# A two-layer hybrid decoder trunk on one core: the gates of all three mixer branches ahead of the first branch's product

## Chip, cores and metric

One Trainium2 chip, one of its cores. The metric is the time of one execution on the device in microseconds. The kernel before was timed in three runs: 1636.29, 1632.41 and 1636.13 us, median 1636.13.

## What is computed

Two layers over 256 tokens of width 1024, each a mixer and then a mixture of experts (MoE), both with a residual. The mixer, cut to what matters here:

```
proj = h @ w_in                                   # one input projection; the last 3 x 1024 columns are the gates
y_a = diff_attention(qa, ka, va) @ w_proj_a       # branch A
y_b = conformer_conv(ub) @ w_proj_b + b_proj_b    # branch B: GLU, 31-tap depthwise conv, layer norm, swish
y_c = stick_breaking(qc, kc, vc) @ w_proj_c       # branch C: 8 heads
g = sigmoid(gates)                                # (token, branch, channel)
merged = g[0] * y_a + g[1] * y_b + g[2] * y_c
return merged @ w_out
```

The MoE sends each token to 8 of 64 experts and adds a shared expert. Which experts' weights sit in which place is known only once the router has run.

## The kernel before

Channels lie on the partitions, tokens on the free axis. A mixer's work on TensorE (PE) is, in this order: the front (the projections to q, k, v and the conv's input), then "gates" and "branches" in the order of the string `PLAN` (line 86), then the output projection, then the MoE.

- `gate(br)` (lines 1205 to 1219) computes one branch's gates: eight chunks of 128 channels by 256 tokens, 24 matmuls each, from two 2 MB weight tiles. The weights are split into a rounded and a residual part by ScalarE (ACT, line 681, `WH`) and VectorE (DVE, line 682, `WL`), two such splits a chunk in layer 0, some five pieces ahead of PE. Each pair of chunks ends in a sigmoid (line 1217) into a tile `sg`, of which there are four; the gates of the branch that comes first go into `merged` instead.
- `branch(br)` (lines 1221 to 1272) waits until the branch's output stands in `T` ("oa", "ob" or "oc"), multiplies it by the projection in four quarters, and adds gate times product to `merged` (lines 1250 to 1256). With four `sg` tiles no more than one branch beside the first can have its gates ready.
- PE's and SyncE's (SP) instructions stand in the order in which the program writes them. Those of DVE and ACT are ordered by a scheduler at build time, by priority in the program's order. Each engine works through its queue in that order.
- A planner writes the program (lines 1312 to 1348). `main()` is the mixer's backbone (gates, branches); each of its turns gives the estimated PE and DVE time of the piece just written. After each turn every "side" (attention heads, rope, the conv's norm) writes its next small piece, and "fills" are written for as long as there is credit: single taps of the conv (line 760, 124 in a layer, estimated at 0.41) and parts of the modulation's dot products (line 525, `mod`, 1.2 each), the two in turn where both are open. Credit grows by `rate` x PE time less DVE time; in layer 0 the rate is 1.2 until A's and C's attention are done, then 0.65.
- Where a branch's input isn't ready, main's turn is a `STALL` of (0.6, 0): only sides and fills are written. A gate chunk is a turn of (2.77, 1.2) in layer 0 and (3.1, 0.78) in layer 1, a quarter of A or C in layer 0 one of (3.65, 1.88).
- `attn_c` (line 1038) begins one head of C every three turns of main in layer 0, every five in layer 1; the last head needs seven turns more, and "oc" is set behind it. `conv_norm` (line 784) follows the conv's last tap over seven turns and sets "ob".
- In layer 0, by this plan, gate a and gate c end with turn 42; turns 43 to 56 are STALLs (14) in which the attention of A and C ends and 47 taps of the conv are written, 11 of them inside the norm of A's output; A is written in turns 57 to 60, C in 61 to 64, gate b in 65 to 72, B in 73 to 76. In layer 1, gate b ends with turn 46, turns 47 to 55 are STALLs (9), A is 56 to 59, B 60 to 63, gate c 64 to 71, C 72 to 75; C's last head begins in turn 63 and "oc" is set in turn 69.
- All weights come through one stream in the order of use: 2 MB tiles in five buffers, issued by SP (line 218 for the mixer, line 251 for the experts). A `mod` tile frees its buffer when its dot products are done. In layer 0 the two `mod` tiles behind gate c's are open to the fills once the next weight tile is taken.

Of the kernel before, what the change touches and what calls it, by code (L numbers as in the profile page):

```python
# [11 lines left out]
F32 = mybir.dt.float32  # L12
# [9 lines left out]
P = 128  # L22
D = 1024
KC = D // P
S = 256
# [57 lines left out]
LK = 1  # L83
GATE1 = 4
START1 = (2, 1, 2)
PLAN = ("acACbB", "abABcC")

_ROWS = [("norm_mix_g", 8), ("norm_ffn_g", 8), ("b_mod", 48), ("b_dw", 4), ("conv_ln_g", 4), ("conv_ln_b", 4),
         ("b_proj_b", 8), ("subln_g", 1), ("qn", 2), ("kn", 2), ("c", 8), ("w_dw", 4 * CW),
# [79 lines left out]
def trunk(ctx, tc, A, out, dbg=None):  # L169
# [21 lines left out]
    def bank(tag):  # L191
        if tag == "S":
            turn[0] ^= 1
            tag = f"S{turn[0]}"
        return ps.tile([P, 512], F32, name="ps" + tag, tag=tag, bufs=4 if tag == "A" else 1)
# [74 lines left out]
    for l in range(L):  # L270
        mods = [(ml, b, kh) for ml, b in MODS[l] for kh in range(2)]
        seq = [("in", n, OFF[n]) for f in FRONT[l] for n in (("uba", "ubg") if f == "ub" else (f,))]
        for br in PLAN[l]:
            if br in "abc":
# [216 lines left out]
    def c2(ap, n=2):  # L491
        return ap.rearrange("p (c t) -> p c t", c=n)
# [98 lines left out]
    def mixer_body(l, pool, before=None):  # L591
# [35 lines left out]
        else:  # L627
            order = [o + (hf,) for hf in range(2) for o in seq[:4] if (*o, hf) in pieces(o)]
            del seq[:4]
        for br in PLAN[l]:  # L630
            if br in "abc":
# [89 lines left out]
        def proj_chunk(n, c, b):  # L721
            mm_all(b[:, (c % 2) * S:(c % 2 + 1) * S], ("in", n, c), XG if n in GATES else X)
# [427 lines left out]
        def main():  # L1150
# [6 lines left out]
            for n in FRONT[l]:  # L1157
# [26 lines left out]
                else:  # L1184
                    for q in range(2):
# [8 lines left out]
                        sg = pool.tile([P, 2, S], F32, name="sg", bufs=4)  # L1194
# [6 lines left out]
            gates = {}  # L1201
            split_ = set("abc")
            done_ = [br.lower() for br in PLAN[l] if br in "ABC"]

            def gate(br):
                gates[br] = []
                for q in range(4):
                    b = bank("A")
                    for k in range(2):
                        proj_chunk(f"g{br}{q // 2}", 2 * (q % 2) + k, b)  # L1210
                        if k == 0:
                            yield GH
                    if br == done_[0]:
                        sg = merged[q // 2][:, 2 * (q % 2):2 * (q % 2) + 2]
                    else:
                        sg = pool.tile([P, 2, S], F32, name="sg", bufs=4)
                    se.activation(sg, c2(b), AF.Sigmoid)
                    gates[br].append(sg)
                    yield GH
# [53 lines left out]

            for br in PLAN[l]:
                yield from gate(br) if br in "abc" else branch(br.lower())
# [638 lines left out]
```

## Time and profile before

| | |
|---|---|
| runs | 1632.41 to 1636.29 us, median 1636.13 |
| the profiled execution | 1630.8 us, its span 1629.1 us |
| share of the span | PE 96%, weight loads 64%, DVE 46%, ACT 29% |
| from HBM | 541.23 MB, 333 GB/s over the span |
| mean granted clock of TensorE | 0.978 |

The span holds mixer 0 (to about 320 us), MoE 0, mixer 1 (about 810 to 1127 us) and MoE 1. In the windows below a row gives, for a stretch, each engine's busy time with its number of instructions, the granted clock of TensorE (1.00 is 2.4 GHz, 0.50 is 1.2 GHz), and the share and rate of the DMA engines. A busy PE may be one at the lower clock.

### The profile page before, as it was taken

To read this page: it belongs to the slowest core of one execution; us is meant where nothing else is said; L and a number is where in the kernel's file an instruction comes from. 1 tells how busy PE (TensorE), PEld (TensorE's weight loads), DVE (VectorE), ACT (ScalarE), POOL (GpSimd) and SP (SyncE) were. 2 spreads that over 40 slices of the span, in tenths; PEclk is the share of its full clock that TensorE was granted. 3 is DMA by queue.
4 is the path that set the end of the run, shared out by engine and by line. 5 is a ranking of instruction groups with operands and counts; after the bars stand their busy time and mean duration, and the time that the engine had idled before them with its cause. 6 is when DMAs were issued, how large, how long until landed. Compare 5 with 4: busy or idle time off the path is not lost. (4 is left out here: it accounts for less than half of the span.)

```text
span 1629.1 us, 25483 instructions
## 1 busy us (share of the span) xinstructions
PE 1565.4 (96%) x9710; PEld 1050.0 (64%) x9710; DVE 751.1 (46%) x1866; ACT 469.5 (29%) x911; POOL 2.9 (0%) x26
## 2 busy tenths in 40 slices
PE   6999999999999999999989999999999999999998
PEld 5999879874555454455478888898654555544544
DVE  8899988642222221212259997554322222211122
ACT  3546724421111111111143355244111111111111
POOL 0000000000000000000000000000000000000000
PEclk7999979999999999999989999899999999999999
DMA  9985319959999999999959744246699999999997
GB/s 379 385 326 200 148 56 369 385 217 372 403 412 419 411 414 416 412 419 412 412 237 373 274 178 155 95 198 259 234 357 405 412 419 412 412 417 415 417 412 309
DMA packets 99198, 543.99 MB, mean 334 GB/s; under 512 B 11136, under 2 KB 11776, under 8 KB 56064
## 3 DMA queue, kind: packets, MB, share of 16 engines
q1 hardware_dynamic: 99072, 542.32, 83.2%
q8 instruction: 78, 1.28, 0.3%
q14 instruction: 48, 0.39, 0.1%
HBM read 541.23 MB, written 1.05 MB: 333 GB/s over the span
## 5 line engine op out<-in xcount | busy, mean ns | idle before, releaser
L198 PE MATMUL psT<-w,xe 128*64 128x512 f32 (+2 forms) x1152 | 229.1, 598 | 5.9 <-DMA w<-in_w_dram 5.8
L1652 DVE TENSOR_SCALAR oT<-psG,slot 128x256 fp32r<-128x256 f32 x54 | 26.1, 484 | 404.9 <-PE psG L198 404.9
L198 PE MATMUL psA<-hH,WH 128*128 128x256 f32 x696 | 209.4, 301 | 0.5 <-ACT WH L681 0.5
L681 ACT ACTIVATE WH<-w 128x512 fp32r<-128x512 f32 (+2 forms) x272 | 148.1, 554 | 200.7 <-PE psA L198 183.0
L1695 DVE SCALAR_TENSOR_TENSOR Y<-psS,gt,Y 128x512 fp32r<-128x512 f32 x108 | 81.1, 751 | 266.6 <-ACT Y L1694 266.6
L198 PE MATMUL psA<-hH,WL 128*128 128x256 f32 x696 | 196.8, 283 | 1.3 <-DVE WL L682 1.3
L198 PE MATMUL psA<-hL,WH 128*128 128x256 f32 x696 | 196.4, 282 | 0.4 <-DVE hL L570 0.4
L198 PE MATMUL psT<-wx,xe 128*64 128x512 f32 (+2 forms) x896 | 186.5, 599 | 8.3 <-DMA wx<-in_w_dram 8.3
L682 DVE TENSOR_TENSOR WL<-w,WH 128x512 fp32r<-128x512 f32 (+2 forms) x272 | 157.2, 591 | 57.2 <-ACT WH L681 56.6
L198 PEld LDWEIGHTS psT<-w,xe 128*64 128x64 f32 (+2 forms) x1152 | 73.3, 129 | 142.5 <-issue 121.7
L198 PE MATMUL psA<-room,w 128*128 128x256 f32 x592 | 145.7, 390 | 1.1 <-ACT room L573 1.1
L198 PEld LDWEIGHTS psT<-wx,xe 128*64 128x64 f32 (+2 forms) x896 | 62.2, 130 | 124.4 <-issue 100.3
L1694 ACT ACTIVATE Y<-psS,gt 128x512 fp32r<-128x512 f32 x108 | 74.4, 689 | 221.5 <-PE psS L198 221.4
L198 PEld LDWEIGHTS psA<-hH,WH 128*128 128x128 f32 x696 | 131.8, 189 | 4.0 <-ACT WH L681 1.7
L198 PEld LDWEIGHTS psA<-hL,WH 128*128 128x128 f32 x696 | 131.9, 190 | 2.8 <-DVE hL L570 0.7
L198 PEld LDWEIGHTS psA<-hH,WL 128*128 128x128 f32 x696 | 131.7, 189 | 2.2 <-DVE WL L682 2.1
L1642 ACT ACTIVATE sl<-psT 128x256 f32<-128x256 f32 x54 | 20.7, 384 | 385.2 <-PE psT L198 385.2
L198 PEld LDWEIGHTS psA<-room,w 128*128 128x128 f32 x592 | 109.8, 194 | 17.3 <-issue 2.9
L198 PE MATMUL psA<-oT,Y 128*128 128x256 f32 x864 | 116.0, 286 | 0.8 <-ACT Y L1694 0.8
L525 DVE SCALAR_TENSOR_TENSOR w<-w,room 128x1024 f32<-128x1024 f32 x96 | 115.7, 1220 | 1.1 <-DMA w<-in_w_mod_dram 1.1
L198 PEld LDWEIGHTS psA<-oT,Y 128*128 128x128 f32 x864 | 105.7, 189 | 3.6 <-ACT Y L1694 3.4
L760 DVE SCALAR_TENSOR_TENSOR room<-room,tcol,room 128x256 f32<-128x256 f32 x240 | 104.0, 481 | 0.0
(586 smaller groups left out, 2070.7 us busy)
## 6 DMA issues: line engine op xcount, KB each, us to landing
w<-in_w_dram SPq DMA_DIRECT2D x108, 1024.0 KB, 15.6
w<-in_w_dram SPq DMA_DIRECT2D x192, 512.0 KB, 10.2
wx<-in_w_dram SPq DMA_DIRECT2D x92, 1024.0 KB, 15.0
wx<-in_w_dram SPq DMA_DIRECT2D x144, 512.0 KB, 10.2
w<-in_w_in_dram SPq DMA_DIRECT2D x56, 1024.0 KB, 8.3
w<-in_w_mod_dram SPq DMA_DIRECT2D x48, 1024.0 KB, 9.3
w<-in_w_out_dram SPq DMA_DIRECT2D x8, 1024.0 KB, 8.5
wx<-in_w_dram SPq DMA_DIRECT2D x4, 2048.0 KB, 17.0
```

Of the source, the lines that this page charges most:

```text
L198: pe.matmul(out=o, lhsT=lhsT, rhs=rhs, start=start, stop=stop, skip_group_check=True)
L525: ve.scalar_tensor_tensor(t[:, j], t[:, j], 1.0, crow, op0=OP.mult, op1=OP.mult, accum_out=modv[l][:, c:c + 1])
L681: se.activation(H[:, j:], src, AF.Copy)
L682: ve.tensor_tensor(Lo[:, j:], src, H[:, j:].bitcast(F32), op=OP.subtract)
L760: ve.scalar_tensor_tensor(yv[:, ch], hp[:, ch, w:w + S], wc, yv[:, ch], op0=OP.mult, op1=OP.add)
L1642: se.activation(sl, b[:, 0:FF], AF.Silu)
L1652: ve.tensor_scalar(oT, bg[:, 0:S], slot[:, k_:k_ + 1], None, op0=OP.is_equal)
L1694: se.activation(Y[:, hf], b, AF.Copy, scale=gt)
L1695: ve.scalar_tensor_tensor(Y[:, 2 + hf], b, gt, Y[:, hf].bitcast(F32), op0=OP.mult, op1=OP.subtract)
```

## The change

In both layers the third gate moves from ahead of the last branch's product to behind the second gate. Its four tiles get a name of their own, outside the room that holds `sg`. What is computed is the same; the stream of weights follows the new order.

```
-PLAN = ("acACbB", "abABcC")
+PLAN = ("acbACB", "abcABC")
...
                     if br == done_[0]:
                         sg = merged[q // 2][:, 2 * (q % 2):2 * (q % 2) + 2]
                     else:
-                        sg = pool.tile([P, 2, S], F32, name="sg", bufs=4)
+                        sg = pool.tile([P, 2, S], F32, name="sg" if len(gates) == 2 else "sg3", bufs=4)
```

A small letter is a branch's gate, a capital its product.

## Rows read from the trace of the kernel before

**Rows 1.** The page: the slices of 40.7 us each, busy tenths of DVE, the granted clock, and GB/s moved.
```profile
DVE  8899988642222221212259997554322222211122
PEclk7999979999999999999989999899999999999999
GB/s 379 385 326 200 148 56 369 385 217 372 403 412 419 411 414 416 412 419 412 412 237 373 274 178 155 95 198 259 234 357 405 412 419 412 412 417 415 417 412 309
```
**Rows 2.** Windows: the stretches before the experts of layer 0 and of layer 1 are known, and a stretch of MoE 0. Columns: stretch, its length, then PE, weight loads (PEld), DVE, ACT, POOL busy (x instructions), granted clock, DMA share, GB/s.
```profile
332.00:345.00 13.00, 12.77 (x76) 10.72 (x74) 10.10 (x51) 4.02 (x8) 0.00 (x0) 1.00 0.01 2
...
1138.00:1152.00 14.00, 13.78 (x80) 11.60 (x79) 11.30 (x65) 5.23 (x10) 0.00 (x0) 1.00 0.00 0
...
440.00:600.00 160.00, 157.34 (x954) 82.97 (x948) 36.60 (x84) 27.46 (x50) 0.00 (x0) 1.00 1.02 415
```
**Rows 3.** Windows of mixer 0, same columns: the end of the front with gates a and c; the tail of the attention in three parts; A and C; gate b.
```profile
137.00:201.38 64.38, 64.38 (x482) 57.47 (x483) 61.28 (x161) 48.63 (x91) 0.00 (x0) 1.00 0.39 149
201.38:209.50 8.12, 7.87 (x54) 5.92 (x52) 8.02 (x21) 5.95 (x13) 0.00 (x0) 1.00 0.01 3
209.50:215.20 5.70, 3.29 (x11) 1.75 (x11) 5.70 (x24) 3.16 (x7) 0.00 (x0) 0.50 0.01 1
215.20:227.31 12.11, 12.03 (x40) 7.40 (x41) 9.21 (x21) 2.12 (x5) 0.00 (x0) 0.53 0.00 0
227.31:256.98 29.67, 29.67 (x149) 26.39 (x148) 25.37 (x55) 4.24 (x8) 0.00 (x0) 1.00 0.54 213
256.98:279.95 22.97, 22.97 (x195) 22.94 (x194) 22.59 (x43) 11.01 (x18) 0.00 (x0) 1.00 0.95 381
```
**Rows 4.** The timeline of PE at the end of that tail: start, length, engine, line, operation, tiles and shapes, number, and in brackets the idle time before it with what ended it.
```profile
215.22 0.58 PE L968 MATMUL psT<-ident,rsy 128*4 128x128 f32 x2 [2.43 <-DVE rsy L459]
...
224.47 3.00 PE L198 MATMUL psS<-room,part 128*128 128x256 f32 x8
227.31 7.07 PE L198 MATMUL psA<-room,w 128*128 128x256 f32 x32
...
235.92 10.61 PE L198 MATMUL psA<-room,w 128*128 128x256 f32 x48
```
**Rows 5.** The timeline of DVE: the conv's last tap, the second half of A's output, and the last operation of the conv's norm.
```profile
220.93 0.48 DVE L760 SCALAR_TENSOR_TENSOR room<-room,tcol,room 128x256 f32<-128x256 f32 x1
223.09 0.75 DVE L981 SCALAR_TENSOR_TENSOR room<-room,sub,psS 128x512 f32<-128x512 f32 x1 [1.69 <-PE psS L198]
...
251.12 0.48 DVE L815 SCALAR_TENSOR_TENSOR room<-room,tcol,room 128x256 f32<-128x256 f32 x1
```
**Rows 6.** Windows from the end of gate c to the end of A's output: all instructions, the same columns as in group 3.
```profile
201.38:223.84 22.46, 19.73 (x92) 12.45 (x92) 20.64 (x61) 10.85 (x24) 0.00 (x0) 0.68 0.01 1
```
**Rows 7.** Windows of line 682 alone (the residual splits; DVE busy, x instructions, clock, DMA): over gate b.
```profile
256.98:279.95 22.97, 10.04 (x15) 1.00 0.95 381
```
**Rows 8.** Windows of line 525 alone (the dot products; two records each), the same columns: behind A's output to the end of the conv's norm, and behind that over gate b.
```profile
223.84:251.60 27.76, 9.56 (x16) 0.95 0.48 186
251.60:280.00 28.40, 14.66 (x24) 1.00 0.86 350
```
**Rows 9.** The DMA issues of SP in mixer 0 by the tensor that they read: first issue, time to the last one's end, number.
```profile
160.57 0.80 SPq L218 DMA_DIRECT2D w<-in_w_proj_a_dram  x2
176.27 0.80 SPq L218 DMA_DIRECT2D w<-in_w_proj_c_dram  x2
193.52 38.33 SPq L218 DMA_DIRECT2D w<-in_w_in_dram  x4
242.81 0.80 SPq L218 DMA_DIRECT2D w<-in_w_proj_b_dram  x2
```
**Rows 10.** Windows of mixer 1, all instructions, the columns of group 3: the tail behind gate b in two parts; A; B; gate c.
```profile
1013.40:1018.40 5.00, 4.01 (x26) 2.50 (x26) 2.68 (x5) 2.46 (x6) 0.00 (x0) 1.00 0.93 392
1018.40:1028.90 10.50, 10.33 (x46) 7.52 (x44) 3.50 (x11) 2.40 (x5) 0.00 (x0) 0.66 0.01 2
1028.90:1046.40 17.50, 17.50 (x80) 14.74 (x79) 8.41 (x21) 4.89 (x11) 0.00 (x0) 0.91 0.00 0
1046.40:1060.80 14.40, 14.40 (x116) 13.24 (x114) 12.00 (x25) 5.50 (x11) 0.00 (x0) 1.00 0.78 292
1060.80:1086.80 26.00, 26.00 (x180) 24.31 (x180) 11.52 (x21) 11.71 (x23) 0.00 (x0) 1.00 0.32 122
```
**Rows 11.** The timeline of mixer 1: PE's first 48 records of branch A, and then the steps of C's last head behind its scores: sigmoid, scans, product, copy of the transposed weights, copy of the output, its rounded part, its residual part.
```profile
1028.92 12.15 PE L198 MATMUL psA<-room,w 128*128 128x256 f32 x48
...
1060.97 0.49 ACT L1005 ACTIVATE room<-psS 128x384 f32<-128x384 f32 x1 [0.65 <-PE psS L198]
...
1061.80 1.00 DVE L1012 TENSOR_TENSOR_SCAN room<-room 128x128 f32<-128x128 f32 x2
...
1062.90 0.56 DVE L1013 TENSOR_TENSOR room<-room 128x384 f32<-128x384 f32 x1
...
1070.60 0.49 ACT L935 ACTIVATE room<-psG 128x384 f32<-128x384 f32 x1
...
1077.59 0.38 ACT L1031 ACTIVATE room<-psT 128x256 f32<-128x256 f32 x1 [0.63 <-PE psT L198]
1078.01 0.63 ACT L1233 ACTIVATE oH<-room 128x512 fp32r<-128x512 f32 x1
...
1078.67 0.69 DVE L1234 TENSOR_TENSOR oL<-room,oH 128x512 fp32r<-128x512 f32 x1 [1.39 <-ACT oH L1233]
```

## Prediction

> **What bounds the kernel now.** I read the slices first, then windows stage by stage, then single rows of the stages that the change touches. In the experts' stages memory sets the pace: there the DMA engines move some 415 GB/s and are full [rows 1, 2]. Before each of these stages lie 13 and 14 us in which nothing is moved: the buffers are full, and the stream waits to learn which experts come next [rows 2]. So a mixer that ends earlier starts the experts earlier with the same tiles in place, and a microsecond won or lost in a mixer is one in the total. I cost the mixers alone.
>
> In mixer 0, PE and DVE share the pace while gates and attention run: over gates a and c DVE is busy 61.28 of 64.38 us (95%) [rows 3]. Then gate c is out, and until A starts (201.38 to 227.31) PE has only the attention's remainder, small matmuls in chains through DVE and ACT. The clock falls to 0.50 [rows 3], and one wait alone is 2.43 us [rows 4]. Behind it A, C and gate b run with no gap. In mixer 1 the tail lies behind gate b (1013.4 to 1028.9), with 0.99 us of idle PE (5.00 less 4.01) and the clock at 0.66 [rows 10].
>
> **Layer 0.** Gate b (22.97 us [rows 3]) leaves its place behind C and is written in the first 8 of the 14 waiting turns; 6 remain.
>
> From PE: the tail's work at full clock is busy time times clock: 7.87 + 3.29 x 0.50 + 12.03 x 0.53 = 15.9 us of 25.93 [rows 3]. With gate b in it, 38.9 us in place of 48.9: a gain of 10.0, if nothing else binds.
>
> From DVE: until A's output is finished, 20.64 us of the 22.46 are busy [rows 6]; nothing of gate b's splits or of the dot products is among them beyond one record. Now come ahead of that point gate b's 16 splits, 10.04 for 15 [rows 7], so 10.7; and the two modulation tiles behind gate c, which are opened to the fills by the taking of gate b's weights and so move ahead of A: 8 dot products, 9.56 us, today behind A's output [rows 8]. Sum 20.64 + 10.7 + 9.6 = 40.9 us. At the 95% that DVE reached over gates a and c this is 43 us, at 100% 40.9; A's output is finished at 242.3 to 244.4, not 223.84 [rows 5]: 18.5 to 20.6 later. From there to A's start PE takes 3.47 us now, most of it the conv's mean at half clock (3.00 [rows 4]); at full clock half of that comes back, 1.5. A starts 17.0 to 19.1 us later, and 22.97 are gone behind C: a gain of 3.9 to 6.0. I take 4.7, nearer to the lower end, since 95% is what a row shows; that DVE and not PE decides follows from 40.9 against 38.9. Bounds: 10.0 from PE's rows; below nothing, if the conv comes late (rival 3).
>
> The engines' queues: DVE's splits wait behind taps and dot products, and PE waits for the splits; that is this sum. ACT gets 16 roundings and four sigmoids into a stretch with 10.85 of 22.46 busy [rows 6]; over gate b its whole busy time is 11.01 [rows 3], and it has room for both. SP's queue: gate b's tiles take the places that A's and C's weights have (issued at 160.57 and 176.27), A's take 193.52, and the queue is idle from there to 231 [rows 3, 9], so gate b finds its weights early. C's and B's then wait for buffers of gate b or of the dot products, freed well ahead of 245. POOL's queue gets nothing. The dot products of the next tiles, 14.66 us over gate b now [rows 8], lose that place; they take the 9.56 us that are vacated beside A and C, and the rest goes beside B and the output projection. The four extra tiles cost nothing while running: their last reader is the last branch, and the output projection lies between it and the MoE.
>
> **Matmul busy time or weight loads?** In the part from 215.20 PE is busy 12.03 of 12.11 us, its weight loads only 7.40 [rows 3]. The Trainium skill (Perfetto Trace Analysis, "Identifying the Most-Contended Engine") says that matmul busy time is a bad measure of how full PE is and that weight-load time should be read. By matmul busy time the tail could take in 2.7 us of gate b (25.93 less 7.87 + 3.29 + 12.03); by weight loads (15.07 in all) up to 10.9.
>
> **Layer 1.** Gate c (8 chunks) moves into the tail's nine waiting turns. What comes back: 0.99 us idle, 10.33 x (1 - 0.66) = 3.5 at the lower clock, and 17.50 x 0.09 = 1.6 under A [rows 10]: 6.1 us. DVE, busy 6.18 of these 15.5 us [rows 10], has room here.
>
> But gate c was also the cover for the last head of C. C's heads begin by count of turns; the last begins with the turn behind B, so its whole chain now stands ahead of branch C: sigmoid 0.49, scans 1.00, product 0.56, copies 0.49 and 0.38, split 0.63 + 0.69, sum 4.24 [rows 11], with hand-overs of 0.04 to 0.34 between rows that follow each other, say 0.5, less 0.7 for the first matmuls of C that need no late channel: 4.0 us of idle PE. PE's own part of the chain is only moved. Net +2.1. The clock may fall again there: at least nothing, at most what tail and A lose now, 3.5 + 1.6; I take 1.5, the excess of A's first 48 records (12.15 [rows 11] against 10.61 in mixer 0 [rows 4]). Net +0.6, bounds -3.0 and +2.1.
>
> **Sum.** 4.7 + 0.6 = 5.3 us. The profiled execution of 1630.8 would become 1625.5; it is 5.3 below the median of 1636.1, so from the median I forecast **1630.8**. A measurement tells 0.3% (4.9 us) from no change; the forecast lies just beyond it.
>
> **Rivals.**
> 1. *DVE gives way.* If the dot products slip behind A after all, or DVE runs denser, PE's sum holds: layer 0 gains 10.0 and layer 1 up to 2.1: 12, so 1624. For it: beside gates a and c weight loads fill 57.47 of 64.38 us (89%) [rows 3], so PE is hardly less full than DVE. Against: 95% busy, and the taps come first in program order. 0.16.
> 2. *The wait is only moved.* Layer 0 gains its lower end, 3.9, and layer 1 loses 3.0, as branch C starts behind an idle PE at 1.2 GHz: gain 1, 1635. For it: the clock fell 5 us behind gate b, in work much like the last head's [rows 10]. The Trainium skill (TensorE: Matmul & The Clock Gate, "HAM oscillation") says the same, that a PE left waiting between bursts begins the next burst at the lower clock; the trace agrees, with 0.66 and 0.91 behind that tail. With the nearby lower end of my own range this makes no change. 0.18.
> 3. *The conv comes late for B, in layer 0*: slower. Today 30 us lie between the last tap and "ob" (220.93 to 251.60 [rows 5]), and B starts 28 us after that. After the change the last tap is near 242, "ob" near 272, B near 275: 3 us to spare in place of 28. By the plan's credit the waiting turns filled 19.3 us of taps with 0.8 unused; eight gate turns give 1.2 x 2.77 - 1.2 = 2.12 each, not 0.72, so 31.3 in all, against 19.3 + 9.6 for taps and dot products: 2.4 to spare. If that fails, the taps left over fall into A's turns, where credit is 0.65 x 3.65 - 1.88 = 0.49, one tap a turn, 3.7 us of PE each: from two taps left over on B waits, from about four the sum is lost and more (14.6 late less 3 gives 11.6, less the gain of 5.3: 6 slower, with the clock's fall some 10). Time 1646. 0.16.
>
> **Chances and range.** My forecast with 3 to 8 us of gain has 0.50: 0.28 of it beyond 4.9 us, 0.22 within. Faster: 0.28 + 0.16 = 0.44. Same: 0.22 + 0.18 = 0.40. Slower 0.16. The range takes in rival 1 with 2 us for the spread of the runs, 1622, and above rival 2 and the milder half of rival 3, 1641; about 1 in 10 is left out above, under 1 in 10 below.
>
> **What would show it.** Right: gate b's matmuls from 201 on, interleaved with the attention, A's start at 243 to 247, B's at 273 to 276, no clock at 0.50 for 17 us there; dot products ahead of A; in mixer 1, A's start some 20 us later than now, and 3 to 6 us of idle PE ahead of branch C with its rows of line 1012 and 1234 as releasers. Wrong: a gap ahead of B in mixer 0 that ends on line 815; DVE under 85% busy between 201 and 245; or a time at which the experts' first load waits for buffers and not for the router.

## The result, and the profile after

The changed kernel is slower. Eight runs took 1638.18 to 1648.14 us, median 1641.97; eight of the kernel before, on the same chip, 1629.56 to 1636.29, median 1633.07. The ratio is 1.0057 (95% interval 1.0044 to 1.0070), 9 us: over the 0.3% that a measurement can tell, on the other side of the forecast, and just above the range (1622 to 1641). The profiled execution of the changed kernel took 1638.2 us, the lowest of its eight; its span is 1636.6, the mean granted clock 0.981 (before 0.978).

Windows of mixer 0 of the changed kernel, with the columns of [rows 3]: the front with gates a and c; gate b with the attention; the rest of the tail; A and C in two parts, cut where PE waits; B and the first of the output projection; the rest.

```profile
137.00:201.40 64.40, 64.40 (x482) 57.37 (x481) 61.27 (x154) 49.53 (x92) 0.00 (x0) 1.00 0.48 184
201.40:235.84 34.44, 34.44 (x258) 31.63 (x256) 32.16 (x81) 19.68 (x39) 0.00 (x0) 0.95 0.49 183
235.84:251.21 15.37, 11.56 (x41) 7.07 (x41) 11.72 (x30) 2.77 (x6) 0.00 (x0) 0.67 0.01 1
251.21:271.50 20.29, 15.87 (x83) 13.89 (x81) 18.14 (x45) 1.42 (x3) 0.00 (x0) 0.99 0.56 214
271.50:287.14 15.64, 15.64 (x69) 13.72 (x69) 12.28 (x23) 3.02 (x6) 0.00 (x0) 0.90 0.95 393
287.14:305.00 17.86, 15.84 (x126) 15.30 (x125) 16.48 (x34) 7.97 (x15) 0.00 (x0) 1.00 0.93 372
305.00:328.00 23.00, 23.00 (x187) 22.68 (x185) 9.35 (x17) 9.64 (x18) 0.00 (x0) 1.00 0.58 229
```

Up to the end of gate c nothing has moved: 64.40 us against 64.38 [rows 3]. Then gate b and the tail take 34.44 + 15.37 = 49.8 us, where the tail and gate b apart took 25.93 + 22.97 = 48.9 [rows 3]: the cover bought nothing. A and C take 35.9 us in place of 29.67 [rows 3]; that is the larger loss, 6.3 us. The mark at which a mixer ends is, here and in the expectations below, "the experts' first matmul". The matmul that the times are taken from is the spread of the MoE's norm (`psA<-dg,ones`); the shared expert's own first one stands 2.08 us behind it in both kernels. The mark comes at 331.89, 7.65 us later than before (324.24).

The timeline of PE in the changed kernel shows both places; the lines answer to [rows 4].

```profile
237.46 0.38 PE L968 MATMUL psT<-ident,rsy 128*4 128x128 f32 x2 [1.63 <-DVE rsy L459]
...
240.84 0.87 PE L930 MATMUL psG<-ident,room 128*128 128x128 f32 x3 [2.19 <-DVE room L1013]
...
246.48 3.78 PE L198 MATMUL psG<-room,part 128*128 128x256 f32 x8
...
251.21 3.72 PE L198 MATMUL psA<-room,w 128*128 128x256 f32 x16
...
256.47 10.61 PE L198 MATMUL psA<-room,w 128*128 128x256 f32 x48
271.50 1.20 PE L198 MATMUL psS<-room,ones 128*128 128x128 f32 x4 [4.42 <-DVE modA L534]
272.49 15.01 PE L198 MATMUL psA<-room,w 128*128 128x256 f32 x64
287.14 0.47 PE L198 MATMUL psA<-oH,WH 128*128 128x256 f32 x1
```

Behind gate b the waits and the half clock of the old tail are still there (the conv's mean, which was 3.00 us in [rows 4], is 3.78). Between A and C a new wait stands: 4.42 us, ahead of the four matmuls that spread the conv's norm over the channels, and after it the clock is at 0.90 on the mean of the 15.64 us up to B. C's 64 matmuls stand behind those four in PE's queue.

What PE waits for there is told by the timeline of DVE in the changed kernel. The lines of 450 to 459 are the norm's eleven steps of 0.16 us each (a reciprocal root by three Newton steps), line 481 makes the diagonal matrix that PE waits for (the profile names line 534, the instruction right behind it); 525 is a dot product, 1254 multiplies a quarter of A by its gate.

```profile
256.71 0.15 DVE L450 TENSOR_SCALAR rsv<-psT 128x2 f32<-128x2 f32 x1
...
260.21 0.69 DVE L1254 TENSOR_TENSOR room<-psA,room 128x512 f32<-128x512 f32 x1 [2.07 <-PE psA L198]
260.81 0.16 DVE L452 TENSOR_SCALAR rsy<-rsv 128x2 int32<-128x2 int32 x1
260.88 1.22 DVE L525 SCALAR_TENSOR_TENSOR w<-w,room 128x1024 f32<-128x1024 f32 x1
...
262.02 0.16 DVE L455 TENSOR_TENSOR rst<-rsy 128x2 f32<-128x2 f32 x1
262.10 1.22 DVE L525 SCALAR_TENSOR_TENSOR w<-w,room 128x1024 f32<-128x1024 f32 x1
...
263.24 0.16 DVE L457 SCALAR_TENSOR_TENSOR rst<-rst,rsv 128x2 f32<-128x2 f32 x1
263.31 1.22 DVE L525 SCALAR_TENSOR_TENSOR w<-w,room 128x1024 f32<-128x1024 f32 x1
...
264.46 0.16 DVE L459 SCALAR_TENSOR_TENSOR rsy<-rst,rsy 128x2 f32<-128x2 f32 x1
...
270.93 0.42 DVE L481 TENSOR_TENSOR room<-ident,rsy 128x256 f32<-128x256 f32 x1
```

Read the gaps between the short lines: in nearly every one stands a dot product of 1.22 us. From the norm's first step to its diagonal it takes 14.2 us, with eight dot products in between, and with three instructions of line 1254, one of which waits 2.07 us for PE while the norm's next step stands behind it. Before, it took 8.2, with three dot products:

```profile
236.10 0.16 DVE L450 TENSOR_SCALAR rsv<-psT 128x2 f32<-128x2 f32 x1 [0.99 <-PE psT L198]
...
244.29 0.42 DVE L481 TENSOR_TENSOR room<-ident,rsy 128x256 f32<-128x256 f32 x1
```

PE has 48 matmuls, 10.61 us, to cover this chain in both kernels. A chain of 8.2 us fits under them and one of 14.2 does not. The planner wrote one tile's four dot products in A's first turn, but the next two tiles' only in B's last turn, in the output projection and behind it. DVE's order, however, is set by the scheduler at build time, which takes whatever is ready by its reckoning. Before, the three tiles of the next layer's vectors were issued at 243.71, 257.37 and 260.42 and landed from 255.20 on, behind the norm's steps; now gate b's tiles free their buffers earlier, and they are issued at 209.80, 224.32 and 256.82 (the third as soon as the first one's dot products have freed its buffer) and landed by 217.28, 231.64 and 264.16. So they could be put into the gaps of the chain, and were.

In mixer 1, windows of the changed kernel over gate c with the attention, the rest of it to A, A, B, the stretch to C, and C; they answer to [rows 10].

```profile
1022.60:1054.31 31.71, 31.71 (x212) 28.05 (x210) 12.27 (x22) 14.03 (x30) 0.00 (x0) 1.00 0.36 134
1054.31:1058.40 4.09, 4.09 (x27) 3.16 (x27) 1.84 (x5) 1.10 (x2) 0.00 (x0) 1.00 0.93 389
1058.40:1075.41 17.01, 17.01 (x88) 13.98 (x87) 11.52 (x30) 5.12 (x11) 0.00 (x0) 1.00 0.05 21
1075.41:1087.40 11.99, 11.99 (x101) 11.89 (x99) 8.87 (x16) 5.19 (x9) 0.00 (x0) 1.00 0.01 1
1087.40:1094.59 7.19, 4.41 (x18) 2.67 (x17) 4.04 (x8) 2.51 (x5) 0.00 (x0) 0.70 0.00 0
1094.59:1107.70 13.11, 13.04 (x98) 12.74 (x98) 8.64 (x16) 5.63 (x11) 0.00 (x0) 0.90 0.91 362
```

The tail is at full clock, as forecast. Between B and C stand 7.19 us with 2.78 of idle PE, and C takes 13.11 us at 0.90 (11.7 before). From the end of the conv's last tap to the experts' first matmul mixer 1 takes 134.85 us, against 134.80: in this pair of executions, even.

### The profile page after: what moved, and what is told of

Same layout as the page of the kernel before. It is cut to its first block, busy times and chain, and to the rows that moved or that the text cites. A ratio compares the mean times of both kernels' runs of the same rounds, so it can differ in the third digit from the quotient of the medians.

```text
span 1636.6 us, 25484 instructions
## 1 busy us (share of the span) xinstructions
PE 1563.3 (96%) x9710; PEld 1051.0 (64%) x9710; DVE 751.2 (46%) x1866; ACT 468.9 (29%) x911; POOL 2.9 (0%) x26
```

## The experiments

**Which mixer?** Each order alone.

```
-PLAN = ("acbACB", "abcABC")
+PLAN = ("acbACB", "abABcC")      # e1
+PLAN = ("acACbB", "abcABC")      # e2
```

> Only mixer 0 has the new order; mixer 1 keeps the old one. Theory D (the loss lies in mixer 0, where VectorE sets the pace and its instructions are queued in a worse order): mixer 0 ends 7.6 us later than in the kernel before, mixer 1 takes no longer, time 1640 to 1642, ratio 1.004 to 1.006. Rival M1 (mixer 1's idle PE and lower clock ahead of branch C make the loss): ratio under 1.002.

> Only mixer 1 has the new order. Theory D: the 6 us that its tail gives back and the waits ahead of branch C cancel, ratio 0.999 to 1.001, 1631 to 1635. Rival M1: ratio 1.003 or more. If the four extra tiles alone cost something, both this run and the one of mixer 0 are slower.

Measured: mixer 0 alone 1636.61, ratio 1.0029 (1.0014 to 1.0044); mixer 1 alone 1635.48, ratio 1.0019 (1.0006 to 1.0032). Neither theory holds alone: both lose, 4.7 and 3.1 us, and together they make most of the whole. The 2.77 us of idle PE ahead of C are there in e2, 4.42 ahead of the norm's spread in e1. e1's profiled execution took 1644.52 us, well above the median, so its rows overstate the loss. That both lose is also what the last sentence of e2's expectation gave for the four extra tiles; the traces rule it out. In the kernels made from the changed one a mixer in the old order has these tiles too, and it takes no longer for them: mixer 1 (from the end of the conv's last tap) 131.6 to 131.7 us with them in e13, e16 and e17 and without them in e5, e10 and e18; mixer 0 (from the conv's first tap) 221.5 and 221.6 with them in e2 and e11, 220.7 to 222.8 without them.

**The dot products, held back.** In e3 they cannot be put among the norm's steps; in e4 the two tiles ahead of A are held back as well.

```
+    LATE_DOTS = ((1, 0), (1, 1))               # e4: ((0, 5), (1, 0), (1, 1)), and (0, 5) in the condition below
+    one_late = const.tile([P, 1], F32, name="one_late")
...
-            ve.scalar_tensor_tensor(t[:, j], t[:, j], 1.0, crow, ...
+            ve.scalar_tensor_tensor(t[:, j], t[:, j], one_late if (l, blk) in LATE_DOTS else 1.0, crow, ...
...
-                while not mods or "crow" not in T:
+                while not mods or "crow" not in T or (mods[0][0] > l) and "ob" not in T:
...
             T["ob"] = yv
+            if l == 0:
+                ve.tensor_scalar(one_late, yv[:, 3, 0:1], 0.0, 1.0, op0=OP.mult, op1=OP.add)
...
+MOD_AT = ((2, 3, 4, 5, 6, 8, 16, 16, 16, 16, 16, 18), ...     # e4 only; 11, 11 before
```

> The changed kernel; the dot products of layer 1's modulation tiles read a one that is written behind the conv's norm, so that none of them can be queued between the norm's steps. Their loads and their number stay. Theory D: the 4.42 us for which PE waits in branch A, and the lower clock behind it, go; A and C together take 29.7 to 31 us in place of 36.1; B and the output projection take at most 2 us longer for the dot products they now share with; 1635 to 1638, ratio to before 1.001 to 1.003. Rival W (the wait comes from the late start of the conv's norm or from transfers, and not from the dot products): over 3 us of idle PE remain, 1641 to 1643.

> As the run before, and the two tiles whose dot products came ahead of branch A (9.8 us of VectorE beside gate b) are loaded behind branch B's weights and held back like the others. Theory D (gate b as a cover buys nothing, because VectorE is full beside it): A starts at 242 to 246 us in place of 251.2, mixer 0 ends 4 to 8 us ahead of the kernel before unless the dot products hold up B and the output projection; 1626 to 1632, ratio 0.996 to 1.000. Rival L (the chain of small steps at the attention's end sets A's start, whatever VectorE does beside it): A still starts at 249 or later.

Measured: e3 1620.97, ratio 0.9936 (0.9919 to 0.9952), 14 us less than the theory allowed; e4 1630.53, ratio 0.9988 (0.9974 to 1.0002). In e3 A and C do take 29.8 us again, with no wait in them. But mixer 0 is only 5.8 us shorter than in the changed kernel; the rest of the gain lies in the experts' stages, which the edit does not touch. There the transfers ran at 423 GB/s in e3 and in e4, where the kernel before has 415 [rows 2] and the changed one too. The new constant `one_late` is the only thing ahead of the weight tiles in memory that differs: it moved the first of them from 22240 to 22272 bytes in its partition, and the others, in steps of 16384, with it. So both runs mixed two things, and the next four took them apart.

In e4 A starts 142.5 us behind the conv's first tap, against 147.4 in the changed kernel and 145.6 in e3: 3 us for 9.8 us of VectorE taken out of the way. On the trace's own clock A starts at 249.85, as rival L had it; but the conv's first tap comes 3.5 us later there than in the changed kernel, and with that taken off it is 246.3, between the theory and the rival. The dot products, all behind the norm now, and the later loads cost more than that: from B to the experts' first matmul e4 takes 60.6 us, the kernel before 44.3. Against e5 below, which has the same addresses, e4 is 0.6% slower. The timeline of PE in e4, its waits alone:

```profile
295.02 0.67 PE L198 MATMUL psA<-room,w 128*128 128x256 f32 x2 [3.65 <-DMA w<-in_w_out_dram]
297.99 0.58 PE L198 MATMUL psA<-mH,WH 128*128 128x256 f32 x1 [2.31 <-ACT WH L684]
300.45 0.58 PE L198 MATMUL psA<-mH,WL 128*128 128x256 f32 x1 [1.66 <-DVE WL L685]
302.95 0.58 PE L198 MATMUL psA<-mH,WH 128*128 128x256 f32 x1 [0.64 <-ACT WH L684]
307.15 0.58 PE L198 MATMUL psA<-mH,WL 128*128 128x256 f32 x1 [3.41 <-DVE WL L685]
```

**The address alone.** One constant of 4 bytes, in the kernel before (e5) and in the changed one (e6); and a larger one in the kernel before, 9 numbers wide (e14, 64 bytes further), 72 wide (e15, 288 bytes) and, last of all runs, 24 wide (e18, 96 bytes).

```
+    pad_ = const.tile([P, 1], F32, name="pad_")      # e14: [P, 9], e15: [P, 72], e18: [P, 24]
+    ge.memset(pad_, 0.0)
```

> The kernel before, with one more constant of 4 bytes ahead of the weight tiles and nothing else: all weight tiles start 32 bytes higher, at a multiple of 64. The two runs whose dot products were held back had such a constant by accident, and their experts' stages moved 423 GB/s in place of 415. Theory S (the address of the weight tiles sets the rate of the transfers): 423 GB/s, both experts' stages some 7 us shorter each, 1617 to 1622, ratio 0.990 to 0.993. Rival O (the new order of the dot products shortens the experts' stages): 415 GB/s, ratio 0.998 to 1.002.

> The changed kernel with the same constant of 4 bytes. Theory S: 423 GB/s, 1625 to 1630; against the kernel before with that constant the change keeps its loss of 7 to 10 us, with 4.4 us of idle PE in branch A. Rival O: 415 GB/s, 1640 to 1643.

> The kernel before with the weight tiles 64 bytes higher, at an odd multiple of 32 bytes as in the kernel before. If the multiple of 64 sets the rate: 415 GB/s between 440 and 600 us. If any shift does: 423.

> The kernel before with the weight tiles 288 bytes higher, at a multiple of 512. If a multiple of 64 is enough: 423 GB/s. If larger multiples help further: over 424 GB/s.

> The kernel before with the weight tiles 96 bytes higher, at 22336 bytes, a multiple of 64 and not of 128. The two fast addresses, 22272 and 22528, are multiples of 256 as well. If a multiple of 64 is enough: 422 to 423 GB/s between 440 and 600 us. If it takes 128 or more: 414 to 415, or a rate between.

Measured: e5 1618.91, ratio 0.9928 (0.9912 to 0.9945); e6 1625.67, 0.9957 (0.9944 to 0.9970); e14 1631.14, e15 1620.64 and e18 1628.95, one run each. Windows of 160 us inside MoE 0, columns as in [rows 2], for e5, e14, e15 and e18:

```profile
440.00:600.00 160.00, 157.34 (x974) 82.42 (x966) 36.58 (x84) 27.45 (x50) 0.00 (x0) 1.00 1.02 423
```

```profile
440.00:600.00 160.00, 157.35 (x962) 82.83 (x952) 36.58 (x84) 27.45 (x50) 0.00 (x0) 1.00 1.02 414
```

```profile
440.00:600.00 160.00, 157.34 (x978) 82.27 (x972) 36.37 (x85) 27.45 (x50) 0.00 (x0) 1.00 1.02 422
```

```profile
440.00:600.00 160.00, 157.36 (x974) 82.42 (x964) 36.59 (x84) 27.40 (x50) 0.00 (x0) 1.00 1.02 415
```

The last column decides: weight tiles at 22272 and 22528 bytes (multiples of 256) are filled at 422 to 423 GB/s; at 22240 and 22304 (odd multiples of 32) and at 22336 (a multiple of 64, none of 128) at 414 to 415. The four have the instructions of the kernel before and differ in the constant alone, which moves every tile behind it. The chip is not the cause: e5 to e8 ran on one, e5 and e6 at 423, e7 at 415. Theory S holds in that the address sets the rate, and rival O falls; but the multiple of 64, which the expectations took for the rule, is not enough. Whether 128 is was not tried. With the tiles moved in both kernels the change still costs 6.8 us by the medians of e6 and e5, 4.7 by their ratios; e6's expectation had 7 to 10.

**The dot products without the move, and gate b spread.** e7 is e3 with the one in the mixer's pool, behind the weight tiles. e8 adds waiting turns between gate b's chunks.

```
-    one_late = const.tile([P, 1], F32, name="one_late")
+                late_[0] = pool.tile([P, 1], F32, name="one_late")      # where "ob" is set
...
                     yield GH
+                    if l == 0 and br == "b":       # e8; behind the first chunk of a pair too, from the third pair on
+                        yield STALL
```

> The dot products of the next layer's tiles behind the conv's norm as before, but with the one kept in the mixer's pool, so that the weight tiles stay where the kernel before has them. Theory S and D together: 415 GB/s, mixer 0 some 6 us shorter than in the changed kernel, 1634 to 1638, ratio 1.000 to 1.003. Rival O: 1619 to 1623.

> As the run before, and in mixer 0 a waiting turn follows most of gate b's chunks, so that gate b is spread over all of the attention's remaining turns. Theory C (gate b is used up early, and the last head's chain of small steps and the conv's mean stand bare behind it at half clock): branch A starts 4 to 8 us earlier than in the run before, measured from the conv's first tap, and the time falls by as much, to 1628 to 1632. Rival D (VectorE's sum of work sets A's start): A starts within 2 us of the run before.

Measured: e7 1637.04, ratio 1.0028 (1.0018 to 1.0038), by the ratios 4.7 us less than the changed kernel, at 415 GB/s. The timeline of DVE in e7, the same eleven steps:

```profile
258.38 0.16 DVE L450 TENSOR_SCALAR rsv<-psT 128x2 f32<-128x2 f32 x1 [0.99 <-PE psT L198]
258.57 0.17 DVE L452 TENSOR_SCALAR rsy<-rsv 128x2 int32<-128x2 int32 x1
258.78 0.16 DVE L455 TENSOR_TENSOR rst<-rsy 128x2 f32<-128x2 f32 x1
...
260.54 0.42 DVE L481 TENSOR_TENSOR room<-ident,rsy 128x256 f32<-128x256 f32 x1
```

They take 2.2 us to the diagonal, not 14.2; no dot product stands among them, and no instruction of line 1260 (1254 in the changed kernel). PE waits nowhere in A and C, which take 29.8 us: rival W falls. e8: 1633.39, ratio 1.0000 (0.9988 to 1.0012), 3.7 us less again; A starts 143.3 us behind the first tap in place of 145.7, between what theory C and rival D gave. The later runs with the same mixer 0 lean to theory C: the spread gave 140.4 (e12), 141.8 (e17) and 141.9 (e13), where six profiles without it have 145.5 to 147.5. The last head's chain has work beside it now, but VectorE, in e8 busy for 43.5 of the 46.2 us from 203 up to A, leaves little more to win; that it holds A as well is argued from this.

**VectorE's part.** The 20 dot products cut to 8 columns, in the changed order (e9) and the old (e10).

```
+            n = 8 if (l, blk, fh) in CUT else D       # the five tiles of mixer 0 behind gate c's
+            ve.scalar_tensor_tensor(t[:, j, 0:n], t[:, j, 0:n], 1.0, crow[:, 0:n], ...
```

> The changed kernel, in which 20 dot products of mixer 0 (five modulation tiles, 24.5 us of VectorE) read 8 of their 1024 columns: they stay in their places and take next to nothing, and what they feed is wrong from mixer 1 on, so only mixer 0 is read. From the conv's first tap to the experts' first matmul the changed kernel took 228.1 us and the one before 220.7. Theory V (the new order leaves VectorE no place for these 24.5 us): 215 to 218 us, and at least 2 us less than the kernel before with the same cut. Rival P (TensorE, busy for 216 of the 220.7 us already, gains nothing from the new order even with VectorE free): within 1 us of the kernel before with the same cut.

> The kernel before with the same cut of 24.5 us of VectorE in mixer 0. Theory V: 218 to 220.5 us from the first tap to the experts' first matmul, since most of these dot products lie beside gate b, where TensorE sets the pace. Rival P: the same as the changed kernel with the cut, within 1 us.

Measured, one execution each, from the first tap to the experts' first matmul: 214.5 us in the new order, 222.8 in the old. With the dot products it was 228.1 against 220.7. So the order that loses 7.4 us wins 8.2 when VectorE has 24.5 us less to do; each is a little outside the span of its expectation (215 to 218, 218 to 220.5), on the side that widens the difference. Single profiles of one mixer differ by some 2 us: the old order, dot products and all, took 220.7 to 222.8 us in seven of them (mean 221.8), the new one 228.1 to 229.0 in three (mean 228.7). On these means the order loses 6.9; e9 lies 7.3 below the old order's mean, and e10 within its range, so in the old order the cut wins nothing. Windows of e9, over gate b (with the last 1.7 us of gate c ahead of it), the rest of the tail, and A and C:

```profile
201.40:235.65 34.25, 34.25 (x272) 31.72 (x271) 32.37 (x84) 21.26 (x41) 0.00 (x0) 1.00 0.33 125
235.65:244.04 8.39, 8.39 (x41) 5.28 (x39) 5.76 (x27) 2.52 (x6) 0.00 (x0) 0.80 0.55 201
244.04:273.82 29.78, 29.78 (x151) 26.50 (x149) 18.41 (x53) 4.44 (x9) 0.00 (x0) 1.00 0.74 297
```

The rest of the tail is 8.39 us with PE never idle, in place of 15.37; taps and splits that stood behind dot products now come earlier (the conv's last tap ends 132.9 us behind the start of its first, in place of 141.4). Theory V holds, rival P falls.

**Mixer 1's last head, and all parts together.** e11 is e2 with the heads of C every four turns; e12 is e8 with that and with the constant of e5.

```
-C_GAP = (3, 5)
+C_GAP = (3, 4)
```

> Only mixer 1 has the new order, and branch C's heads begin every 4 turns in place of every 5, so that the last one no longer starts behind branch B. Theory T (the new order of mixer 1 costs what the last head's chain, now bare ahead of C, costs: 2.8 us idle and 1.5 at the lower clock): the wait of 2.77 us ahead of C goes, 4 us less than the run with mixer 1 alone, 1630 to 1633, ratio 0.997 to 1.000. Rival U (mixer 1's loss lies elsewhere, as in the earlier stages of that mixer): within 1.5 us of it.

> All that the runs pointed to, in one kernel: the new order in both mixers, the weight tiles 32 bytes higher, the next layer's dot products behind the conv's norm, gate b spread over the waiting turns, branch C's heads every 4 turns in mixer 1. If the parts add up: 1633.4 less 14 for the address and 4 for mixer 1, 1615, ratio 0.988 to 0.991, some 3 us below the kernel before with the address alone (1618.9).

Measured: e11 1641.35, ratio 1.0051 (1.0032 to 1.0071), by the ratios 5 us worse than e2, not 4 better. The wait for the head ahead of C is gone, but a new one stands ahead of B, and two smaller ones are left ahead of C, for the rounding of its input; the timeline of PE:

```profile
1079.54 0.58 PE L198 MATMUL psA<-oH,WH 128*128 128x256 f32 x1 [3.03 <-ACT oH L1233]
...
1096.32 0.39 PE L198 MATMUL psA<-oH,WH 128*128 128x256 f32 x1 [1.13 <-ACT oH L1233]
1097.96 0.39 PE L198 MATMUL psA<-oL,WH 128*128 128x256 f32 x1 [1.26 <-DVE oL L1234]
```

The conv's norm is now the one that comes late: it ends at 1079.61, as B starts (in the changed kernel 1069.45, 6 us ahead of B). Behind it the clock falls (0.67 from 1079.54 to 1088.50), and B's first 48 matmuls take 8.9 us in place of 6.0. Theory T is half right (the head's chain did make that wait) and its forecast wrong. The gate that had covered both had been spent by then; what made the norm late was not followed further. e12, with the same fault, takes 1622.55, ratio 0.9939 (0.9916 to 0.9961), and not the 1615 expected: mixer 0 217.3 us, 3 less than before, mixer 1 5 more from its conv's last tap. It does not beat the kernel before with its tiles moved (e5).

**Mixer 0 mended, mixer 1 as before.** e16 is e7, e17 is e8 and e13 is e8 with e5's constant, each with mixer 1 in the old order.

```
+PLAN = ("acbACB", "abABcC")
```

> Mixer 0 in the new order with the next layer's dot products behind the conv's norm, mixer 1 in the old order, weight tiles where the kernel before has them. With mixer 1 new this was 1637.0, ratio 1.0028. Theory M: 1632 to 1634, ratio 0.999 to 1.001. Rival N: 1636 to 1638.

> Mixer 0 in the new order with the next layer's dot products behind the conv's norm and gate b spread; mixer 1 in the old order; weight tiles where the kernel before has them. Theory Q (the new order gains in mixer 0 once the dot products are out of the norm and the cover reaches the last head): 1627 to 1630, ratio 0.996 to 0.999, and mixer 0 some 1 to 3 us shorter than before. Rival (it only comes back to even, as the dot products now hold up the output projection): ratio 0.999 to 1.001.

> Mixer 0 in the new order, with the next layer's dot products behind the conv's norm and gate b spread over the waiting turns; mixer 1 in the old order; the weight tiles 32 bytes higher. Theory M (mixer 1's new order costs 3 to 5 us, and mixer 0's new order gains once the dot products are out of its way): mixer 1 takes 167 us from its first tap to the experts' first matmul in place of 172, 1612 to 1616, ratio 0.988 to 0.990, below the kernel before with the address alone (0.9928). Rival N (mixer 1's order does not matter, the rest is lost elsewhere): 1618 to 1621.

Measured: e16 1635.43, ratio 1.0024 (1.0009 to 1.0039), between the two theories; e17 1629.86, ratio 0.9970 (0.9957 to 0.9984); e13 1614.56, ratio 0.9896 (0.9868 to 0.9924). e17 wins 0.3% without the address: mixer 0's new order together with the dot products held back and gate b spread. What holding them back would do in the old order was not run; e10, where they are cut there, wins nothing. e13 is the fastest of all, 1.0% below the kernel before, most of it from the address.

The stages in one table, in us: mixer 0 from the conv's first tap to A, to B and to the experts' first matmul; mixer 1 from the end of the conv's last tap to the experts' first matmul. Each row is one execution; e8 and e17, with one program in mixer 0, differ by 3.3 us there. To compare A's starts, 23.0 for gate b have to be added where it comes behind C (the first row: 146.8).

| kernel | to A | to B | mixer 0 | mixer 1 |
|---|---|---|---|---|
| before | 123.8 | 176.4 | 220.7 | 134.8 |
| after | 147.4 | 183.4 | 228.1 | 134.9 |
| e5, before, tiles moved | 124.4 | 177.0 | 222.6 | 131.7 |
| e6, after, tiles moved | 145.6 | 183.0 | 229.0 | 136.7 |
| e7, dots behind the norm | 145.7 | 175.4 | 222.3 | 136.6 |
| e8, and gate b spread | 143.3 | 173.0 | 222.4 | 136.5 |
| e9, after, dots cut | 138.8 | 168.6 | 214.5 | 136.3 |
| e10, before, dots cut | 124.4 | 177.0 | 222.8 | 131.7 |
| e17, e8 with mixer 1 old | 141.8 | 171.5 | 219.1 | 131.7 |

In e17 to B 4.9 us are won, and 3 of them are lost again up to the experts: the dot products that were held back now stand beside the output projection, where PE waits 1.63 and 1.93 us for splits of ACT and DVE.

## Why the prediction failed, point by point

**"They take the 9.56 us that are vacated beside A and C".** This step failed, and it is the largest error: the dot products' new place was costed at nothing, because VectorE's sum of work fits there. It fits as a sum; but a chain of eleven short steps runs there that PE waits for, and the scheduler put a dot product of 1.22 us into its gaps. The 29.7 us of A and C, left unchanged in the forecast, became 35.9: 4.42 idle and most of the rest the clock behind it. With the dot products held back (e7) the stage takes 29.8 and the kernel, by the ratios, 4.7 us less. The prediction had even named the conv's norm as what B waits for, and forecast its end at 272 (measured 276.05); it did not see that PE waits inside it, with C's matmuls queued behind those four. It followed the weights of A, C and B through SP's queue, but not the next layer's tiles behind them, which came 34 us earlier (issued from 209.80 on in place of 243.71) and so were ready for the gaps.

**"A starts 17.0 to 19.1 us later".** This is the second step that failed. It started 23.9 later, and 21.7 to 23.7 in e1, e3, e6, e7 and e16 (against the same 23.0 of gate b that are gone behind C; from the first tap, 145.5 to 147.5 against 123.8). VectorE's sum was nearly right: 40.9 us of work forecast up to the end of A's output; 42.96 us busy in the 45.93 us from 201.40 to 247.33 in the trace. It came out by another way than forecast: none of the 42.96 us are dot products. The eight ran earlier still, at 176.83 to 198.8 beside gate c (9.82 us), where VectorE is busy 61.27 of 64.40 us with them as it was without, and 22 of the conv's taps moved from there into the stretch. A's output was finished at 247.33, 23.5 us later and not 18.5 to 20.6, and from there to A's start PE took 3.88 us, not 2.0. What was left out is the second half: gate b is used up at 235.84, and the last head's chain and the conv's mean stand bare behind it, with 1.63 and 2.19 us of idle PE and the clock at 0.67. So the sign "no clock at 0.50 for 17 us there" did not come either: a mean of 0.67 over 15.37 us, of the two levels, is some 10 us at 0.50. Both parts showed on the chip: spreading gate b brings A 2.4 us forward (e8 against e7; 3.8 to 5.3 in the three later profiles), cutting the dot products 8.6 (e9).

The two readings of PE's room that the prediction set side by side can be judged now. From 201.40 to 235.84 PE is busy for all 34.44 us, its weight loads for 31.63; gate b took 11.5 us longer there than by itself, and the tail became 10.6 shorter. The Trainium skill (Perfetto Trace Analysis, "Identifying the Most-Contended Engine") would have weight loads read and not matmul busy time. By weight loads up to 10.9 us of gate b fitted into the tail, by matmul busy time 2.7. With VectorE busy for 32.16 of these 34.44 us the trace went below both, to -0.9; with its load cut, e9 starts A 8.5 us earlier than e10 with gate b added, nearer to the reading by weight loads.

**Layer 1, "net +0.6".** In the pair of profiled executions it is even, but that is luck of both: the kernel before met a low clock in its tail that most others did not, and the changed kernel's was the shortest of its kind. The 3.5 us to be "given back" at the lower clock were there in that execution and not in most others. The same tail, with the same instructions, in e5 (the kernel before but for a constant), and A behind it:

```profile
1008.00:1023.73 15.73, 14.57 (x93) 10.99 (x92) 8.66 (x25) 6.31 (x14) 0.00 (x0) 1.00 0.36 135
1023.73:1041.29 17.56, 17.56 (x79) 14.74 (x79) 8.70 (x23) 4.88 (x11) 0.00 (x0) 0.90 0.00 0
```

The clock is at 1.00 where [rows 10] have 0.66. From the conv's last tap mixer 1 in its old order took 131.6 to 131.7 us in six profiles (e5, e10, e13, e16, e17, e18), 134.7 to 134.8 in three (before, e14, e15) and 137.8 in one (e1). In the new order it took 136.1 to 136.7 in seven and 134.9 in one (139.8 in e11 and e12, whose heads begin earlier). So the new order costs 3 us on the mean, the lower end of the bounds given; by the times 3.1 (e2), 4.9 between e8 and e17 in their ratios, and 0.7 between e7 and e16. The idle time ahead of C was 2.78 where 4.0 was forecast, and C's loss to the clock 1.4 where 1.5 was; the term that failed is the 3.5 that the tail was to give back.

**The sum.** Layer 0 was to gain 4.7 us and lost 7.4 in the profiles: 5.6 of the 12.1 us between are A's start (23.9 for the 18.3 that the gain of 4.7 stands for), 6.2 the stage of A and C. With the means of several profiles, 6.9 in mixer 0 and 3.1 in mixer 1, the loss comes to 10.0, where the times show 9.

**The rivals.** Rival 2 had layer 1 right, a loss of 3.0 from the wait ahead of C, but left layer 0 a gain of 3.9. Rival 3 was on the right side, by a mechanism that did not occur in layer 0: the last tap ended at 245.2, ahead of A, and B found its input ready 11 us before it started. It did occur in mixer 1 of e11. Rival 1, with layer 0 gaining 10.0, is near what e9 shows, but only with VectorE's work cut.

**What stays open.** e16 should have been even with the kernel before and is 0.24% slower; in its profile mixer 0 took 224.2 us against 222.3 in e7 with the same program there, so single profiles do not tell where these 3.9 us lie. Why the experts' stages differ by 1 to 2 us between kernels with one address was not looked into, nor why the clock falls in mixer 1's tail in some executions.

## What to carry to other kernels

When a stage moves, follow what becomes ready earlier, not only what is moved: an order made at build time can put long instructions that are ready into the gaps of a chain of short ones, and a sum of busy time does not show it. Cover must last as long as the chain that it covers; used up early, it leaves the slowest part bare. A dip of the clock in one profile is a gain to be had only if a second execution shows it too, and an experiment that adds a tile ahead of others needs one more that adds the tile alone.

## What the hardware showed that was not expected

The rate at which weights arrive depends on the address of their tiles: 422 to 423 GB/s at multiples of 256 bytes in the partition, 414 to 415 at three addresses that are multiples of 32 or 64 only. With it the time falls by 13.7 us of 1632.6 by the medians of e5, by 11.8 by its ratio, more than the change under study moved. And the same instructions meet TensorE's lower clock in one execution and not in another: mixer 1's tail at 0.66 before and at 1.00 in e5, worth 3 us. It does not go with the address: e10, e16 and e17 have the weight tiles where the kernel before has them and mixer 1 as short as in e5. No kernel was profiled twice.
